# Encoder with seven-product feed-forward blocks: the first product of a pair is handed to the third one's bank by a copy on ScalarE

## The chip, the cores and the metric

The kernel runs on one core of one Trainium2 chip. The metric is the device time of one execution in microseconds, given as the median of three runs. A core has five engines that matter here: TensorE (PE) multiplies matrices and writes PSUM, VectorE (DVE), ScalarE (ACT) and GpSimd (POOL) work element by element, and SyncE (SP) issues most DMAs. Each has a queue of its own that it works through in order, and they wait for one another through semaphores.

## The reference

A two-layer encoder on 512 tokens of width 1024, in fp32. Each layer has two gated feed-forward blocks with an attention mixer and a cross-attention on 256 memory tokens between them:

```
def swiglu(x, wg, wu, wd):
    return (jax.nn.silu(x @ wg) * (x @ wu)) @ wd
...
for layer in range(2):
    g, wg, wu, wd = ffn1[layer]
    h = h + 0.5 * swiglu(rmsnorm(h, g), wg, wu, wd)
    ... h = h + mixer(rmsnorm(h, mix_g)), h = h + memory_xattn(rmsnorm(h, mg), rmsnorm(mem, sg))
    g, wg, wu, wd = ffn2[layer]
    h = h + 0.5 * swiglu(rmsnorm(h, g), wg, wu, wd)
```

The hidden width is 2816, which is 22 groups of 128 channels, worked on as 11 pairs of groups. Only the feed-forward blocks contain the change. There are four of them, at 0 to 330, 760 to 1050, 1050 to 1330 and 1740 to 2068 us of the span.

## The kernel before, in words

**Precision.** An fp32 operand is split in two parts of TensorE's fp32r type: a high part that ScalarE rounds (L457, `wh` or `sh`) and a low part that VectorE gets by subtraction (L458, `wl` or `sl`). A product is then three passes of matmuls, high x high, high x low, low x high. Tokens and hidden values have such parts too: `xh`, `t1h` to `t3h` and their low parts for the tokens, `hh` and `hl` (L379, L380) for the hidden values, `th` and `tl` (L385, L386) for sums of hidden values.

**Seven products.** The gate and up multiplication of a pair of hidden groups is done by the Strassen-Winograd scheme: the operands are cut in quarters, and seven products of quarters with some sums replace eight products. One product is `product` (L481), 24 matmuls of 128x256 into one PSUM bank of 128x512 fp32. Its two halves are gate and up. Pair 0 of each block, the plain pair, is done without the scheme (`plain_pair`, matmuls at L331), and pairs 1 to 10 in seven products. Where the text speaks of a block's first pair, pair 1 is meant, the first in seven products.

A pair p runs through these functions, each of which issues one or two products:
- `open_pair`: product with the tokens "11" into a fresh bank `y`. ScalarE copies it out to `gu` (L523).
- `sum_pair`: product with t1 into a bank `z`; product with t2, which accumulates on `y`. ScalarE copies `y` out (L541).
- `cross_pair`: product with the tokens "21" into a third bank `x`. VectorE adds `x` to the copy that L523 made (L550). Then a product with t3 accumulates on `y`, and ScalarE copies it out (L557), from which VectorE takes `z` (L558).
- `close_pair`: product with t4 on `y`, copied out at L574, and product "22" on `z`. VectorE multiplies by `R`, the factor of the rmsnorm (L609), ScalarE does the Silu (L610), VectorE multiplies by up (L611, L612). It is called after the next pair's `open_pair`.

`gu` is the result of a pair in SBUF, two tiles of 128x1024, one for each half of the tokens. `corner(pair, b, half)` is the piece for group b. There are four such tiles in all.

**The plain pair's end.** `plain_end` runs after the first `open_pair`: VectorE multiplies the two gate banks by `R` (L355), ScalarE does the Silu (L361), VectorE multiplies by the two up banks (L363).

**PSUM.** There are eight banks, four under the tag `pa` and four under `pb`. The plain pair holds three of `pa` (gate and up of its first group, gate of its second) and one of `pb`.

**Down projection.** It runs in three chunks of 8, 8 and 6 hidden groups. The second chunk, `down_seven`, is done in seven products too, in two units; `gain` (L628) adds each result to the residual stream `x` on VectorE, in two pieces of 128x256. It begins with the unit's first product, whose last quarter needs `hh` and `hl` of the newest pair. A unit's first, second and further products go through a bank `y`, and its third goes into a fresh bank `x`, as in `cross_pair`; `gain` runs after each of them. The other chunks (`down`, L707) are plain matmuls.

**What sets the order.** TensorE's order is the order of the program text. The other engines' instructions are placed by a scheduler from estimated times. `high_priority` brings an instruction forward in it, and `behind` puts one after a named other.

## Time and profile before

| | |
|---|---|
| median of three runs | 2066.76 us (2066.62 to 2070.43) |
| profiled execution, its own time | 2068.93 us |
| its span, first to last instruction | 2067.1 us |
| TensorE busy | 2027.3 us, 98% |
| VectorE busy | 1607.1 us, 78% |
| ScalarE busy | 1144.7 us, 55% |
| GpSimd busy | 375.3 us, 18% |
| granted TensorE clock, mean | 0.998 |

How to read it: all times inside the profile count from the span's start. "Busy" is time in which an engine works on an instruction, and a wait is idle time, put down to the instruction on another engine that released it. In the stretch views a row is the stretch, its length, then busy time and count of instructions for PE, PEld (TensorE's loading of weights), DVE, ACT and POOL, then the granted clock, the share of the DMA engines, and GB/s. In the waits a row is the waiting engine and line, what released it, and then the total in us, the count and the longest. In a timeline a row is start, length, engine and line, then what is written from what; a bracket gives idle time before it and the releaser.

### The profile page before, as it was taken

Reading aid. Unit: us, or ns where it says so; the run is one execution under the profiler, and the core shown is the slowest. Engines: PE = TensorE matmul, PEld = TensorE weight load, DVE = VectorE, ACT = ScalarE, POOL = GpSimd, SP = SyncE. Lnnn points to the kernel's source line nnn. Section 1 sums busy time; section 2 is a strip of 40 time slices with the busy share of each in tenths; the row PEclk is TensorE's granted clock in tenths of the full one; section 3 lists DMA queues with packets and bytes.
Section 4 is the critical chain, followed back from the end, with each engine's and each line's share of the span. In section 5 each row is a group of like instructions: output and inputs, shape, how many; then the busy total and the mean of one; then the engine's idle time right before and its main releaser. Section 6 shows DMA issues by size and latency. Waiting matters only on the chain.

```text
span 2067.1 us, 34071 instructions
## 1 busy us (share of the span) xinstructions
PE 2027.3 (98%) x13426; PEld 1836.5 (89%) x13426; DVE 1607.1 (78%) x2470; ACT 1144.7 (55%) x1718; POOL 375.3 (18%) x335
## 2 busy tenths in 40 slices
PE   8999999999999999999999999999999999999999
PEld 7989998887778889899989899988888888989997
DVE  8858987579876789599789679884668777958976
ACT  6525554465686565264555355454778665635543
POOL 1101003345432210000020000113453112000000
PEclk9999999999999999999999999999999999999999
DMA  7837565222232257376557465734223324746572
GB/s 229 214 112 184 163 166 179 94 77 72 67 128 77 72 161 213 103 197 161 156 156 191 133 173 145 211 124 154 82 88 120 100 81 125 194 130 175 162 193 95
DMA packets 89584, 292.32 MB, mean 141 GB/s; under 512 B 10064, under 2 KB 13264, under 8 KB 89424
## 3 DMA queue, kind: packets, MB, share of 16 engines
q1 hardware_dynamic: 75600, 239.81, 34.6%
q0 software_dynamic: 13824, 50.34, 13.9%
q8 instruction: 105, 1.72, 0.3%
q14 instruction: 55, 0.45, 0.1%
HBM read 283.82 MB, written 6.29 MB: 140 GB/s over the span
## 4 chain that ended last, share of the span: by engine, by line
PE 86%; DVE 9%; ACT 2%; issue 1%; DMA 1%; POOL 0%; SPq 0%; DVEq 0%; ACTq 0%; POOLq 0%
PE ps_pa L481 29%; PE ps_pb L481 12%; PE ps_pa L816 11%; PE ps_pa L707 6%; PE ps_pb L707 6%; PE ps_pa L767 4%; PE ps_pa L331 3%; PE ps_pb L922 2%; PE ps_pa L1362 2%; PE ps_pb L974 1%; PE ps_pa L1213 1%; PE ps_pb L767 1%; PE ps_pb L947 1%; DMA mem<-memT 1%; PE ps_pa L1132 1%
## 5 line engine op out<-in xcount | busy, mean ns | idle before, releaser
L164 ACT ACTIVATE wh<-wf 128x1024 fp32r<-128x1024 f32 (+2 forms) x179 | 181.2, 1014 | 250.2 <-PE ps_pa L707 68.5
L457 ACT ACTIVATE wh<-s 128x1024 fp32r<-128x1024 f32 x124 | 132.1, 1065 | 156.4 <-PE ps_pa L481 59.8
L166 DVE TENSOR_TENSOR wl<-wf,wh 128x1024 fp32r<-128x1024 f32 (+2 forms) x137 | 161.1, 1179 | 48.2 <-ACT wh L164 46.3
L458 DVE TENSOR_TENSOR wl<-s,wh 128x1024 fp32r<-128x1024 f32 x124 | 151.6, 1222 | 50.2 <-ACT wh L457 48.0
L457 ACT ACTIVATE wh<-wf 128x1024 fp32r<-128x1024 f32 x104 | 110.4, 1062 | 97.4 <-PE ps_pa L481 57.5
L458 DVE TENSOR_TENSOR wl<-wf,wh 128x1024 fp32r<-128x1024 f32 x104 | 126.9, 1220 | 8.2 <-ACT wh L457 3.7
L502 POOL DMA_DIRECT2D s<-l_ffn_wq x40 | 35.1, 878 | 519.5 <-DMA s<-l_ffn_wq 418.7
L166 POOL TENSOR_TENSOR wl<-wf,wh 128x1024 fp32r<-128x1024 f32 x42 | 101.9, 2425 | 150.9 <-ACT wh L164 140.3
L816 PE MATMUL ps_pa<-wh,xh 128*128 128x512 f32 x384 | 123.6, 403 | 0.0
L816 PE MATMUL ps_pa<-wh,xl 128*128 128x512 f32 x384 | 119.9, 394 | 0.0
L816 PE MATMUL ps_pa<-wl,xh 128*128 128x512 f32 x384 | 119.5, 392 | 0.0
L481 PE MATMUL ps_pa<-xh,wh 128*128 128x256 f32 x672 | 103.8, 276 | 0.0
L481 PE MATMUL ps_pa<-xh,wl 128*128 128x256 f32 x672 | 103.7, 276 | 0.0
L481 PE MATMUL ps_pa<-xl,wh 128*128 128x256 f32 x672 | 103.6, 276 | 0.0
L457 ACT ACTIVATE sh<-s 128x1024 fp32r<-128x1024 f32 x68 | 72.2, 1062 | 49.2 <-PE ps_pa L481 27.5
L231 POOL TENSOR_TENSOR acc<-acc,sq 128x512 f32<-128x512 f32 (+1 forms) x37 | 51.0, 1379 | 255.9 <-ACT sq L230 205.1
L458 DVE TENSOR_TENSOR sl<-s,sh 128x1024 fp32r<-128x1024 f32 x68 | 83.0, 1221 | 14.6 <-ACT sh L457 14.5
L481 PEld LDWEIGHTS ps_pa<-xh,wh 128*128 128x128 f32 x672 | 89.5, 188 | 0.6
L481 PEld LDWEIGHTS ps_pa<-xl,wh 128*128 128x128 f32 x672 | 88.8, 188 | 0.0
L481 PEld LDWEIGHTS ps_pa<-xh,wl 128*128 128x128 f32 x672 | 88.7, 188 | 0.0
L816 PEld LDWEIGHTS ps_pa<-wh,xl 128*128 128x128 f32 x384 | 72.9, 190 | 16.2
L816 PEld LDWEIGHTS ps_pa<-wl,xh 128*128 128x128 f32 x384 | 72.7, 189 | 16.0
(416 smaller groups left out, 5845.5 us busy)
## 6 DMA issues: line engine op xcount, KB each, us to landing
wf<-l_ffn_wq SPq DMA_DIRECT2D x120, 512.0 KB, 4.3
s<-l_ffn_wq SPq DMA_DIRECT2D x80, 512.0 KB, 5.5
s<-l_ffn_wq POOLq DMA_DIRECT2D x80, 512.0 KB, 7.3
wf<-l_w_in SPq DMA_DIRECT2D x48, 512.0 KB, 3.5
wf<-l_ffn_wd SPq DMA_DIRECT2D x32, 512.0 KB, 4.0
wf<-l_ffn_wdq SPq DMA_DIRECT2D x24, 512.0 KB, 3.4
wf<-l_ffn_wd SPq DMA_DIRECT2D x32, 384.0 KB, 3.1
s<-l_ffn_wdq SPq DMA_DIRECT2D x16, 512.0 KB, 4.9
```

Source lines behind the costliest of these rows:

```text
L164: self.leading = nc.scalar.activation(wh[:, sl], w[:, sl], AF.Copy)
L166: eng.tensor_sub(wl[:, sl], w[:, sl], wh.bitcast(F32)[:, sl])
L231: self.summed = (eng or nc.gpsimd).tensor_add(acc[:, :n], acc[:, :n], sq[:, :n])
L331: nc.tensor.matmul(p, w[a][:, k * P:(k + 1) * P], xs[k][c], start=k == order[0] and a == c == 0, stop=k == order[-1] and a == 1)
L457: self.leading = nc.scalar.activation(h, t, AF.Copy)
L458: self.parted = nc.vector.tensor_sub(l, t, h.bitcast(F32))
L481: self.nc.tensor.matmul(bank[:, sl], w[a][:, o:o + P], xs[k][b], start=first and z == a == b == k == 0, stop=z == a == 1 and k == KB // 2 - 1,
L707: self.nc.tensor.matmul(bank, w[a][:, j * P:(j + 1) * P], h, start=j == a == e == 0, stop=j == nb - 1 and (a, e) == ops[-1])
L767: nc.tensor.matmul(banks[dd], a[:, o:o + P], parts(k)[b], start=k == first and a is wh and b == 0, stop=k == last and a is wl)
L816: nc.tensor.matmul(banks[i], xs[k][a][:, i * P:(i + 1) * P], w[b][:, kk * 512:kk * 512 + 512], start=k == a == b == 0, stop=k == KB - 1 an ...
L922: nc.tensor.matmul(bank[:, o:o + n], a, b[:, :n], start=c == 0, stop=c == len(ops) - 1)
L1362: nc.tensor.matmul(p, ws[z][a][:, k * P:(k + 1) * P], xs[k][b], start=k == order[0] and a == b == 0, stop=k == order[-1] and a == 1)
```

## The change

In a pair, the first product's result is no longer copied to `gu` and added to there. ScalarE copies the bank `y` into a new bank `x` under the tag `pa`, right after the first product; the third product then accumulates on `x` instead of starting it; and ScalarE copies `x` to `gu`. VectorE's addition goes. Both `gu` tiles of a pair are now taken in `sum_pair`. In `down_seven` each unit's first result is copied to `x` in the same way, under the tag `pa` for the first unit and `pb` for the second, and `gain` is called once after the third product instead of after the first and the third. The diff, in full:

```diff
@@ -519,8 +519,8 @@
         pair.y = self.bank("pa")
         pair.w11, w = self.raw_operand(p, 0)
         self.product(pair.y, w, self.tokens("11"), True)
-        self.gu_half(pair)
-        self.nc.scalar.copy(self.corner(pair, 0, 0), self.halves(pair.y))
+        pair.x = self.bank("pa")
+        self.nc.scalar.copy(pair.x, pair.y)
         return pair
 
     def sum_pair(self, pair):
@@ -538,16 +538,15 @@
             f.lowered = self.parted
         self.product(pair.y, w, xs, False)
         self.gu_half(pair)
+        self.gu_half(pair)
         nc.scalar.copy(self.corner(pair, 0, 1), self.halves(pair.y))
 
     def cross_pair(self, pair, after=None):
         nc, f, p = self.nc, self.f, pair.p
         with self.behind(f.lowered if p == 1 else None):
             pair.w12, w = self.raw_operand(p, 1)
-        x = self.bank("pa")
-        self.product(x, w, self.tokens("21"), True)
-        c = self.corner(pair, 0, 0)
-        nc.vector.tensor_add(c, c, self.halves(x))
+        self.product(pair.x, w, self.tokens("21"), False)
+        nc.scalar.copy(self.corner(pair, 0, 0), self.halves(pair.x))
         if after is not None:
             self.full_sum(pair)
             after()
@@ -640,7 +639,9 @@
             units.append(t)
         for t in units:
             self.product(t.y, t.w, B["11"], False, range(n - 1, n))
-            self.gain(t.u, t.y, 0, 0)
+            t.x = self.bank("pb" if t.u else "pa")
+            with self.tc.high_priority():
+                nc.scalar.copy(t.x, t.y)
 
         def low(t):
             t.z = self.bank("pb")
@@ -656,10 +657,9 @@
             self.gain(t.u, t.y, 0, 1)
 
         def cross(t):
-            x = self.bank("pa")
             t.w12, w = self.raw_operand(t.p, 1)
-            self.product(x, w, B["21"], True)
-            self.gain(t.u, x, 0, 0)
+            self.product(t.x, w, B["21"], False)
+            self.gain(t.u, t.x, 0, 0)
 
         def left(t):
             w = self.left_sum(t.p)
```

TensorE's instructions and their order are the same, but for the tag of one bank in `down_seven`. The orders of SyncE and GpSimd are the same. Those of ScalarE and VectorE differ in the feed-forward blocks alone. Two places follow as the queues stand, the second on two engines. A row is the source line, the operation, what is written from what, its size, and in brackets the engines and DMA queues that it waits for. `s_384` and the like are sums of two weight quarters, loaded by DMA with addition; `wf` is a plain weight quarter. The line numbers of the changed kernel differ by one from L541 on (L542 for L541, L556 for L557).

ScalarE at the first pair of the first block, before:

```order
L457 ACTIVATE wh<-wf 128x1024 [waits DMAHW5_49,PE_49,Activation_49]
L523 COPY gu<-ps_pa 128x512 [waits PE_49]
L457 ACTIVATE sh<-s_384 128x1024 [waits DVE_49]
L457 ACTIVATE wh<-s_486 128x1024 [waits DMASW1_49,PE_49,Activation_49]
L457 ACTIVATE sh<-wf 128x1024 [waits DMAHW6_49,DVE_49,PE_49]
L541 COPY gu<-ps_pa 128x512 [waits PE_49]
L361 ACT_TABLE_LOAD
L361 ACTIVATE gs<-gs 128x1024 [waits DVE_49]
```

And in the changed kernel:

```order
L457 ACTIVATE wh<-wf 128x1024 [waits DMAHW5_49,PE_49,Activation_49]
L457 ACTIVATE sh<-s_384 128x1024 [waits DVE_49]
L457 ACTIVATE wh<-s_486 128x1024 [waits DMASW1_49,PE_49,Activation_49]
L523 COPY ps_pa<-ps_pa 128x512 [waits DVE_49]
L361 ACT_TABLE_LOAD
L361 ACTIVATE gs<-gs 128x1024 [waits DVE_49]
L457 ACTIVATE sh<-wf 128x1024 [waits DMAHW6_49,PE_49,Activation_49]
L542 COPY gu<-ps_pa 128x512 [waits PE_49]
```

The first result's copy stood behind one conversion and waited for TensorE alone; it now stands behind three, ahead of the Silu's table load, and waits for VectorE. In the other nine pairs it waits for TensorE.

VectorE at the start of `down_seven` in the second block, before (L377, L378, L382 and L383 make the sums `t` of hidden quarters, L653 a sum of weight quarters):

```order
L458 TENSOR_TENSOR wl<-wf,wh 128x1024 [waits DMAHW3_49,PE_49,Activation_49]
L377 TENSOR_TENSOR t<-gs 128x256 [waits DVE_49]
L550 TENSOR_TENSOR gu<-gu,ps_pa 128x512 [waits PE_49]
L458 TENSOR_TENSOR wl<-s_10028,wh 128x1024 [waits DMASW7_49,Activation_49]
L378 TENSOR_TENSOR gs<-gs 128x256 [waits DVE_49]
L653 TENSOR_TENSOR s_10028<-s_10028,wf 128x1024 [waits DVE_49]
L382 SCALAR_TENSOR_TENSOR t<-gs 128x256 [waits DVE_49]
L380 TENSOR_TENSOR hl<-gs,hh 128x1024 [waits Activation_49]
```

And in the changed kernel:

```order
L458 TENSOR_TENSOR wl<-wf,wh 128x1024 [waits DMAHW3_49,PE_49,Activation_49]
L377 TENSOR_TENSOR t<-gs 128x256 [waits DVE_49]
L378 TENSOR_TENSOR gs<-gs 128x256 [waits DVE_49]
L458 TENSOR_TENSOR wl<-s_10026,wh 128x1024 [waits DMASW7_49,PE_49,Activation_49]
L382 SCALAR_TENSOR_TENSOR t<-gs 128x256 [waits DVE_49]
L654 TENSOR_TENSOR s_10026<-s_10026,wf 128x1024 [waits DVE_49]
L380 TENSOR_TENSOR hl<-gs,hh 128x1024 [waits Activation_49]
L383 SCALAR_TENSOR_TENSOR t<-t,gs 128x256 [waits DVE_49]
```

The addition L550 and, some rows on, the additions of the first products are gone; L378 and L382 stand one or two places earlier, and `hl` still comes behind the sum of the weights. In the first block `hl` stands ahead of that sum in the changed kernel.

ScalarE at the same place, before:

```order
L541 COPY gu<-ps_pa 128x512 [waits PE_49]
L457 ACTIVATE wh<-s_10028 128x1024 [waits DMASW7_49,DVE_49,PE_49]
L379 ACTIVATE hh<-gs 128x1024 [waits DVE_49,Activation_49]
L385 ACTIVATE th<-t 128x768 [waits DVE_49]
L457 ACTIVATE sh<-s_10028 128x1024 [waits PE_49]
L457 ACTIVATE wh<-wf 128x1024 [waits DMAHW4_49,PE_49,Activation_49]
```

And in the changed kernel:

```order
L542 COPY gu<-ps_pa 128x512 [waits PE_49]
L457 ACTIVATE wh<-s_10026 128x1024 [waits DMASW7_49,PE_49,Activation_49]
L549 COPY gu<-ps_pa 128x512 [waits PE_49]
L379 ACTIVATE hh<-gs 128x1024 [waits DVE_49,Activation_49]
L385 ACTIVATE th<-t 128x768 [waits DVE_49]
L457 ACTIVATE sh<-s_10026 128x1024 [waits PE_49]
L644 COPY ps_pa<-ps_pa 128x512 [waits PE_49,Activation_49]
L457 ACTIVATE wh<-wf 128x1024 [waits DMAHW4_49,PE_49]
L644 COPY ps_pb<-ps_pa 128x512 [waits PE_49]
```

The copy of `x` to `gu` (L549) has come in ahead of `hh`, and the two copies of first products (L644) behind `th`.

## The prediction

> **What bounds the kernel now.** I began with the page's totals, then cut the span into its six stages, then asked TensorE alone what it waits for.

> ```profile
> span 2067.1 us, 34071 instructions
> PE 2027.3 (98%) x13426; PEld 1836.5 (89%) x13426; DVE 1607.1 (78%) x2470; ACT 1144.7 (55%) x1718; POOL 375.3 (18%) x335
> ```

> TensorE is busy for 98% of the span, and the change alters neither the number nor the shape of its matmuls. VectorE, which loses work, is at 78%, and its work is worth only what TensorE waits for it. So I look for the waits, and the stages in which they lie. The first column of the second view is the stretch, then its length, then busy time by engine.

> ```profile
> 0.00:330.00 330.00, 316.79 (x2392) 300.05 (x2393) 262.61 (x350) 173.62 (x214) 31.35 (x40) 1.00 0.62 174
> 760.00:1050.00 290.00, 288.76 (x2273) 277.53 (x2272) 235.92 (x290) 149.04 (x169) 18.65 (x21) 1.00 0.59 162
> ...
> PE ps_pa L481 <- DVE hl L380: 3.7, 4, 0.9
> PE ps_pa L481 <- ACT gu L541: 2.7, 1, 2.7
> ...
> PE ps_pa L481 <- ACT sh L457: 1.3, 1, 1.3
> ...
> PE ps_pa L481 <- DVE wl L458: 1.1, 4, 0.4
> ```

> L481 is the matmul of the seven-product scheme, the only code that the change touches. In the second feed-forward block (760 to 1050 us) TensorE is idle for 1.24 us of 290. In the whole run L481 waits 3.7 + 2.7 + 1.3 + 1.1 = 8.8 us. Nobody waits for the addition L550 or the first copy L523 on TensorE's side. Little can be won, then; the question is whether the change makes a wait.

> **What is removed and added.** The prices of the operations, minimum/median/maximum in ns:

> ```profile
> L523 ACT COPY gu<-ps_pa x40: 557/567/576, 35.6 to 2008.6; 128x512 f32<-128x512 f32 x40
> L550 DVE TENSOR_TENSOR gu<-gu,ps_pa x40: 678/680/689, 48.2 to 2022.2; 128x512 f32<-128x512 f32 x40
> L628 DVE TENSOR_TENSOR x<-x,ps_pa x80: 414/415/425, 233.8 to 1983.9; 128x256 f32<-128x256 f32 x80
> ```

> VectorE loses 40 additions of 0.68 us and 16 of the 80 + 32 pieces of 0.41 us at L628 (two units, two pieces, four blocks): 34 us. ScalarE gains 40 + 8 copies: 48 x 0.57 = 27 us, on an engine that is 55% busy. In the steady pairs both lie beside TensorE: a pair is seven products of 2.72 us, 19 us, with 11 to 13 us of ScalarE in it, so 0.57 us more fits; I cost them at zero there. If that cover were gone, 40 x 0.57 = 23 us would appear. The copy from PSUM into PSUM is in no row. Its nearest rows are L523 (same source, destination SBUF, 0.57) and, from the other side, L550's 0.68, which also ends a bank. I take 0.57, with 0.45 to 0.70 as bounds: four times 0.12 is 0.5 us in the sum.

> **Where a wait is made: the first pair of each block.** The first pair's copy needs a bank of the tag pa for the third product, ahead of its time. There are four. Three hold the plain pair's gate and up results, and the fourth the pair's own first product. The order of ScalarE says it: this copy waits for VectorE, all other pairs' copies for TensorE. The bank is freed by L355, the multiplication of a gate bank by R. The second block in order of time (columns: start, length in us, engine, line):

> ```profile
> 761.07 0.57 ACT L523 COPY gu<-ps_pa 128x512 f32<-128x512 f32 x1
> ...
> 763.48 0.62 PE L481 MATMUL ps_pa<-t2h,sh 128*128 128x256 f32 x4
> ...
> 765.67 1.28 DVE L355 TENSOR_TENSOR gs<-ps_pa,R 128x512 f32<-128x512 f32 x2
> ...
> 766.37 1.07 ACT L457 ACTIVATE sh<-wf 128x1024 fp32r<-128x1024 f32 x1 [2.02 <-DVE gs L355]
> ...
> 766.62 0.62 PE L481 MATMUL ps_pa<-xh,wh 128*128 128x256 f32 x4
> ...
> 769.34 0.62 PE L481 MATMUL ps_pa<-t3h,wh 128*128 128x256 f32 x4
> 769.34 1.22 DVE L458 TENSOR_TENSOR wl<-s,wh 128x1024 fp32r<-128x1024 f32 x1
> ...
> 770.61 0.73 PE L481 MATMUL ps_pa<-t3h,wl 128*128 128x256 f32 x4 [0.20 <-DVE wl L458]
> 771.18 0.63 PE L481 MATMUL ps_pa<-t3h,wh 128*128 128x256 f32 x4
> ```

> Today the first result is read out at 761.07, and the product with t2, which accumulates on the same bank, starts at 763.48. Tomorrow it must wait until the copy has read that bank. The copy starts when today's row at 766.37 does, which waits for the same L355, and TensorE follows. What such a release costs is seen in the first block, where a late copy of 0.56 us held L481:

> ```profile
> 169.53 0.56 ACT L541 COPY gu<-ps_pa 128x512 f32<-128x512 f32 x1
> ...
> 170.15 0.74 PE L481 MATMUL ps_pa<-t3h,sh 128*128 128x256 f32 x4 [2.73 <-ACT gu L541]
> ```

> TensorE starts 0.06 after the copy's end, and its first group takes 0.12 longer (0.74 instead of 0.62). So: 766.37 + 0.57 + 0.06 = 767.00; six groups take 769.34 - 766.62 = 2.72, plus 0.12; the next product starts at 769.84 instead of 766.62. That is 3.2 us late. VectorE's order up to L355 is the same as before, and ScalarE has nothing else ahead of the copy that ends later. The other three blocks, first row L355, second row the product behind t2:

> ```profile
> 39.90 1.28 DVE L355 TENSOR_TENSOR gs<-ps_pa,R 128x512 f32<-128x512 f32 x2
> ...
> 40.83 0.62 PE L481 MATMUL ps_pa<-xh,wh 128*128 128x256 f32 x4
> ...
> 1095.35 1.28 DVE L355 TENSOR_TENSOR gs<-ps_pa,R 128x512 f32<-128x512 f32 x2
> ...
> 1097.21 0.62 PE L481 MATMUL ps_pa<-xh,wh 128*128 128x256 f32 x4
> ...
> 1762.54 1.28 DVE L355 TENSOR_TENSOR gs<-ps_pa,R 128x512 f32<-128x512 f32 x2
> ...
> 1763.47 0.62 PE L481 MATMUL ps_pa<-xh,wh 128*128 128x256 f32 x4
> ```

> In the second block the way from L355's start to the next product is 769.84 - 765.67 = 4.17. So 39.90 + 4.17 - 40.83 = 3.2, 1095.35 + 4.17 - 1097.21 = 2.3, 1762.54 + 4.17 - 1763.47 = 3.2. Sum of the four: +12.0 us.

> Behind the waiting copy on ScalarE stand the table load, the Silu L361 and the next pair's conversion. The conversion needs a buffer that t2 reads, so it is late with TensorE and not because of the copy. Silu ends about 769.3, before VectorE's L363 uses it (row order, near 772). I cost these at nothing.

> What the delay takes away: in the product with t3, TensorE today loses time on wl (769.34 to 771.18 is 1.84 for three groups worth 1.36, so 0.48, of which 0.20 is the idle time shown). wl does not move, ending at 770.56, and t3 comes 2.3 to 3.2 us later. All four such waits go: 1.1 us of idle time in the view of waits, plus 4 x 0.28 for the restarts: -2.2 us.

> **The down projection in seven products.** Here TensorE waits four times for hl, the low part of the last hidden pair. The second block:

> ```profile
> 946.93 1.06 ACT L457 ACTIVATE wh<-s 128x1024 fp32r<-128x1024 f32 x1 [1.13 <-PE ps_pa L481]
> ...
> 947.31 0.42 DVE L377 TENSOR_TENSOR t<-gs 128x256 f32<-128x256 f32 x1
> ...
> 947.65 0.68 DVE L550 TENSOR_TENSOR gu<-gu,ps_pa 128x512 f32<-128x512 f32 x1
> ...
> 951.19 1.22 DVE L380 TENSOR_TENSOR hl<-gs,hh 128x1024 fp32r<-128x1024 f32 x1
> 951.26 0.28 PE L481 MATMUL ps_pa<-hh,sh 128*128 128x256 f32 x1
> ...
> 952.46 0.38 PE L481 MATMUL ps_pa<-hl,sh 128*128 128x256 f32 x1 [0.92 <-DVE hl L380]
> ```

> Only one matmul at 951.26 can run, and the next, due about 0.1 later, starts at 952.46: 1.1 us lost, 1.2 with the restart. L550 stands in that chain and is removed, and L378 moves to its place, ahead of wl. In the new order the chain is bounded by wh: it ends at 947.99, so wl starts at 948.05. Steps of 1.14 for wl and the sum s, 0.34 for L382 put hl at 950.67 to 951.89, against 952.41 today: 0.5 us won. In the first block hl stands ahead of s, and hh (wh's end 947.99 + copy 0.57 + 1.06 = 949.6) lets it run from about 949.65 to 950.9, before it is needed: 1.2 won. Sum -(1.2 + 3 x 0.5) = -2.7 us. The two new copies of first products must end before the second step; by that order the first ends near 954.9, and the second step starts after 956, so no wait.

> **The clock.** The trace shows what gaps can do to TensorE. In two stretches the column before the last two, the granted clock, falls:

> ```profile
> 496.00:500.00 4.00, 4.00 (x15) 3.25 (x13) 3.89 (x11) 2.34 (x4) 3.49 (x3) 0.57 0.02 4
> 544.00:548.00 4.00, 4.00 (x16) 3.30 (x15) 3.32 (x8) 3.00 (x5) 0.07 (x1) 0.57 0.00 0
> ...
> 169.00:173.00 4.00, 2.85 (x25) 2.85 (x26) 4.00 (x7) 2.56 (x4) 0.88 (x1) 1.00 0.26 101
> ```

> Both lose 4 x 0.43 = 1.7 us, and both follow stretches in attention where TensorE ran only a few transposes. After the 2.73 us wait at 170 the clock stayed at 1.00. The new waits of 3.2 us lie between. I put half a window, 0.9 us, into the sum, with none and three as bounds. [...]

> **Sum.** +12.0 - 2.2 - 2.7 + 0.9 = +8.0 us. Against the profiled execution's 2068.93 that is 2076.9; that execution is 2.2 above the median of the runs, so against the median, 2066.76, it is 2074.8, +0.39%. About 0.2% (4.1 us) is what a measurement of this kernel can tell from no change.

> **Rivals.**
> - Half clock after all three long waits: +7.1 + 3 x 1.7 = +12.2, 2079.0. For it speaks the length of the waits, against it the 2.73 that did nothing.
> - The delay is partly given back in the first block. There L481 waits 2.7 and 1.3 us for ScalarE, which stands behind loads of the memory tokens. If those loads come at fixed times, a pipeline that is 3 us later no longer waits: 4.0 and 2 x 0.28 for restarts, so +8.0 - 4.6 = +3.4, 2070.2. Against it: these loads wait in turn for buffers that the same pipeline frees.
> - ScalarE becomes late in every pair: 40 x 0.57 = 23 more, 2097. Against it 55% load; for it that x's second copy stands ahead of hh in ScalarE's order.
> - The other side: the first copy finds a bank free, as if the plain pair's results had been read out before 763.48, and hl is in time in all four blocks: -4 x 1.2 = -4.8, 2062.0. It is decided by when L355 ends; it ends after t2's start in all four blocks, so I hold it for nearly excluded.

> **Chances.** The forecast 0.62, three slow windows 0.15, given back 0.13, late ScalarE 0.05, the other side 0.03, something else 0.02. The likeliest gives 2074.8, its own range being 2072 to 2078. The range 2070 to 2080 takes in the first two rivals and both ends of the copy's price. Slower 0.83, within 0.2% 0.13, faster 0.04.

> **What the new profile would show.** TensorE's L481 waiting for the copy of L523, four times, 2.3 to 3.4 us each, about 12 in total; the waits on wl gone; the wait for hl smaller, with the first block's gone; SyncE and GpSimd as before. I am wrong if that first wait is missing or under 2 us, if ScalarE's copies hold TensorE in other pairs, or if the copy into PSUM takes far from 0.57.

## The result, and the profile after

The changed kernel takes 2080.69 us (median of 4 runs, 2079.89 to 2082.8), against 2068.6 for the kernel before (median of 4): a ratio of 1.006, 95% interval 1.0042 to 1.0077. It is slower by some 12 us, where 8 were forecast, and the time lies just above the range. (The forecast time stood on a median of 2066.76 for the kernel before; from 2068.6 the same 8 us lead to 2076.6.) The two profiled executions differ by 12.2 us in span, 2079.3 against 2067.1. Of all the runs in this document one lies far off: of the twelve of the kernel with the first pair as before, the profiled one took 11681 us, and it is left out of that kernel's ratio, its trace out of the eleven used below.

The page's totals of the changed kernel:

```profile
span 2079.3 us, 34073 instructions
PE 2033.5 (98%) x13426; PEld 1843.3 (89%) x13426; DVE 1587.0 (76%) x2414; ACT 1170.3 (56%) x1766; POOL 375.3 (18%) x335
```

VectorE is busy for 20 us less and ScalarE for 26 us more. (VectorE's instructions together are 33 us shorter, as forecast; in the record neighbours overlap: in the changed kernel `sl` of L458 runs from 765.59 to 766.81, and `wl` behind it starts at 766.72.) TensorE has the same 13426 matmuls and is busy for 6 us longer, which no count of instructions explains: some of them ran slower (a group of four took up to 1.23 us, below). The waits of L481:

```profile
PE ps_pa L481 <- ACT ps_pa L523: 11.5, 4, 3.4
PE ps_pa L481 <- ACT gu L542: 2.0, 1, 2.0
PE ps_pa L481 <- DVE hl L380: 1.3, 3, 0.4
PE ps_pa L481 <- ACT wh L457: 0.7, 1, 0.7
...
PE ps_pa L481 <- DVE sl L458: 0.3, 1, 0.3
```

The line of the copy by itself, with its duration as minimum/median/maximum in ns, and what it waited for (us, times):

```profile
L523 ACT COPY ps_pa<-ps_pa x40: 570/580/591, 39.9 to 2020.8; 128x512 f32<-128x512 f32 x40
...
  DVE gs L355: 6.3, 4
```

Four waits on the copy of a first result have appeared, and the copy itself waited four times for L355. The waits on wl (1.1 us) are gone, and those on hl fell from 3.7 to 1.3. The copy from PSUM into PSUM takes 0.58. In time order, the second block's first pair, and behind it TensorE's row after the wait in the first, the third and the fourth block:

```profile
767.86 1.28 DVE L355 TENSOR_TENSOR gs<-ps_pa,R 128x512 f32<-128x512 f32 x2
768.58 0.57 ACT L523 COPY ps_pa<-ps_pa 128x512 f32<-128x512 f32 x1 [2.08 <-DVE gs L355]
...
769.20 1.22 PE L481 MATMUL ps_pa<-t2h,sh 128*128 128x256 f32 x4 [3.39 <-ACT ps_pa L523]
...
40.51 0.74 PE L481 MATMUL ps_pa<-t2h,sh 128*128 128x256 f32 x4 [3.00 <-ACT ps_pa L523]
...
1102.46 0.72 PE L481 MATMUL ps_pa<-t2h,sh 128*128 128x256 f32 x4 [2.04 <-ACT ps_pa L523]
...
1772.31 1.23 PE L481 MATMUL ps_pa<-t2h,sh 128*128 128x256 f32 x4 [3.12 <-ACT ps_pa L523]
```

This is the chain that was forecast: L355, the copy 0.72 behind its start, TensorE 0.05 behind the copy's end. But in the second and the fourth block the first group after it takes 1.22 us, not the 0.74 that a group after a wait took before. The stretches around the four places tell why. Each pair of rows is a stretch of 3.41 us with the wait or most of it, and the one behind; the columns are again busy times of PE, PEld, DVE, ACT and POOL, then the granted clock, third from the end:

```profile
38.24:41.65 3.41, 1.14 (x9) 1.15 (x10) 3.41 (x5) 1.75 (x2) 0.00 (x0) 1.00 0.05 18
41.65:45.06 3.41, 3.41 (x18) 3.41 (x17) 3.41 (x6) 1.93 (x3) 0.00 (x0) 0.50 0.01 2
765.28:768.69 3.41, 0.53 (x5) 0.33 (x3) 3.41 (x5) 1.17 (x2) 0.00 (x0) 1.00 0.79 234
768.69:772.10 3.41, 2.90 (x13) 2.90 (x14) 3.41 (x7) 2.80 (x3) 0.00 (x0) 0.50 0.00 0
1099.79:1103.20 3.41, 1.37 (x12) 1.17 (x11) 3.41 (x5) 2.39 (x3) 0.00 (x0) 1.00 0.01 5
1103.20:1106.61 3.41, 3.41 (x18) 3.41 (x18) 3.41 (x7) 0.34 (x2) 0.00 (x0) 0.50 0.02 5
1768.80:1772.21 3.41, 0.39 (x4) 0.19 (x2) 3.41 (x5) 1.58 (x2) 0.00 (x0) 1.00 0.72 219
1772.21:1775.62 3.41, 3.31 (x15) 3.31 (x16) 3.41 (x7) 2.38 (x3) 0.00 (x0) 0.50 0.01 4
```

At all four places TensorE runs for 3.41 us at half clock, even behind the shortest, of 2.04 us in the third block.

Where the 12.2 us lie can be read off by setting each TensorE row of after beside the same row of before and taking the difference of their starts. Starts of the first row of the t2 product, and of the first row behind it:

| block | t2, before | t2, after | later, without the shift that stood | next product, before | next product, after | added within t2 |
|---|---|---|---|---|---|---|
| 1 | 38.08 | 40.51 | 3.17 | 40.83 | 44.85 | 1.59 |
| 2 | 763.48 | 769.20 | 3.55 | 766.62 | 773.38 | 1.04 |
| 3 | 1094.49 | 1102.46 | 2.20 | 1097.21 | 1106.90 | 1.72 |
| 4 | 1760.50 | 1772.31 | 3.28 | 1763.47 | 1776.69 | 1.41 |
| sum | | | 12.2 | | | 5.8 |

The shifts that stood, read at the row just ahead of t2, are -0.74, 2.17, 5.77 and 8.53 (after later than before, where positive). The rest: -1.58 in the t3 products of the first three blocks, -2.16 at hl in them, -1.02 for both in the fourth, -1.5 in the first block beside that, +0.1 at its end, +1.1 in the attention of layer 0 (two stretches of 3.41 us at half clock in a row at 495.6 instead of one), -0.74 at the start. Together 12.2.

### The profile page after: what moved, and what is told of

It reads as the page before. It is cut to its first block, busy times and chain, and to the rows that moved or that the text cites. A ratio compares the mean times of both kernels' runs of the same rounds, so it can differ in the third digit from the quotient of the medians.

```text
span 2079.3 us, 34073 instructions
## 1 busy us (share of the span) xinstructions
PE 2033.5 (98%) x13426; PEld 1843.3 (89%) x13426; DVE 1587.0 (76%) x2414; ACT 1170.3 (56%) x1766; POOL 375.3 (18%) x335
## 3 DMA queue, kind: packets, MB, share of 16 engines
q8 instruction: 105, 1.72, 0.3%
## 4 chain that ended last, share of the span: by engine, by line
PE 86%; DVE 8%; ACT 2%; DMA 2%; issue 2%; POOL 1%; SPq 0%; ACTq 0%; POOLq 0%; DVEq 0%
PE ps_pa L481 29%; PE ps_pb L481 12%; PE ps_pa L816 11%; PE ps_pa L707 6%; PE ps_pb L707 6%; PE ps_pa L767 4%; PE ps_pa L331 2%; PE ps_pb L922 2%; PE ps_pa L1362 2%; PE ps_pb L974 1%; PE ps_pa L1213 1%; PE ps_pb L947 1%; PE ps_pb L767 1%; PE ps_pa L1132 1%; DVE xl L214 1%
## 5 line engine op out<-in xcount | busy, mean ns | idle before, releaser
L457 ACT ACTIVATE wh<-s 128x1024 fp32r<-128x1024 f32 x124 | 132.0, 1065 | 130.2 <-PE ps_pa L481 49.0
L166 DVE TENSOR_TENSOR wl<-wf,wh 128x1024 fp32r<-128x1024 f32 (+2 forms) x137 | 161.1, 1179 | 48.8 <-ACT wh L164 46.8
L458 DVE TENSOR_TENSOR wl<-s,wh 128x1024 fp32r<-128x1024 f32 x124 | 151.6, 1223 | 60.5 <-ACT wh L457 58.0
L457 ACT ACTIVATE wh<-wf 128x1024 fp32r<-128x1024 f32 x104 | 110.7, 1064 | 94.7 <-PE ps_pa L481 40.8
L458 DVE TENSOR_TENSOR wl<-wf,wh 128x1024 fp32r<-128x1024 f32 x104 | 127.0, 1222 | 20.0 <-ACT wh L457 15.1
L166 POOL TENSOR_TENSOR wl<-wf,wh 128x1024 fp32r<-128x1024 f32 x42 | 101.8, 2424 | 151.9 <-ACT wh L164 141.3
L457 ACT ACTIVATE sh<-s 128x1024 fp32r<-128x1024 f32 x68 | 72.3, 1064 | 61.3 <-PE ps_pa L481 33.1
L458 DVE TENSOR_TENSOR sl<-s,sh 128x1024 fp32r<-128x1024 f32 x68 | 83.4, 1226 | 30.2 <-ACT sh L457 30.1
L481 PE MATMUL ps_pa<-xh,wh 128*128 128x256 f32 x672 | 103.9, 277 | 0.0
L481 PE MATMUL ps_pa<-xh,wl 128*128 128x256 f32 x672 | 103.8, 276 | 0.0
L481 PE MATMUL ps_pa<-xl,wh 128*128 128x256 f32 x672 | 103.6, 276 | 0.0
L481 PEld LDWEIGHTS ps_pa<-xh,wh 128*128 128x128 f32 x672 | 89.7, 188 | 0.6
L481 PEld LDWEIGHTS ps_pa<-xl,wh 128*128 128x128 f32 x672 | 88.8, 188 | 0.0
L481 PEld LDWEIGHTS ps_pa<-xh,wl 128*128 128x128 f32 x672 | 88.8, 188 | 0.0
```

The lines of the kernel that those rows point to most:

```text
L166: eng.tensor_sub(wl[:, sl], w[:, sl], wh.bitcast(F32)[:, sl])
L457: self.leading = nc.scalar.activation(h, t, AF.Copy)
L458: self.parted = nc.vector.tensor_sub(l, t, h.bitcast(F32))
L481: self.nc.tensor.matmul(bank[:, sl], w[a][:, o:o + P], xs[k][b], start=first and z == a == b == k == 0, stop=z == a == 1 and k == KB // 2 - 1,
```

## Experiments

The ratios below are to runs of the kernel before that were taken with each group of kernels; their medians were 2069.82 us for the kernels with the free bank, with the first pair as before, with the down projection alone and with L355 earlier, 2070.44 for the last two with shorter waits, and 2069.05 for the others.

**The bank.** The first pair's `x` is taken where a bank is free; the condition on `mem_r` holds in the first block alone:

```diff
-        pair.x = self.bank("pa")
+        pair.x = self.bank("pb" if p == 1 else "pa")
+        if p == 1 and self.mem_r is None:
+            for z in range(2):
+                self.nc.tensor.matmul(pair.x[:, z * 256:z * 256 + 256], w[0][:, :P], self.tokens("11")[0][0],
+                                      start=z == 0, stop=z == 1, skip_group_check=True)
```

> The changed kernel, but the first pair's x comes from the tag pb, where a bank is free, so that its copy need not wait for L355 (in the first block two extra matmuls write that bank ahead of the copy, about 0.5 us). Theory, the missing bank: the four waits on the copy (11.5 us) and the four half-clock windows behind them go, the waits on wl (1.1 us) come back, the wait for hl stays at about 1.3 us; -2.7 us against before plus 0.5 for the two matmuls, 2066.4 against 2068.6. Rival, the copies themselves: a copy in each pair disturbs TensorE or the clock wherever the bank comes from, and the time stays near 2080. Rival in part: only the waits go and the clock still falls, about 2071.

Measured: 2067.03 us, a ratio to before of 0.9987 (0.9979 to 0.9996), the forecast having been 0.9989. No wait on the copy is left in the trace, and none of the first pairs has a window at half clock. So all of the loss hung on that bank, its clock included, and 40 + 8 copies by themselves cost nothing that shows in an interval of 0.0017, 3.5 us. (A wait of 2.6 us behind the memory tokens, which the kernel before has too, has a half-clock window behind it here, at 171.5.)

**The first pair as before.** The rest of the change is kept:

```diff
+        if p == 1:
+            self.gu_half(pair)
+            self.nc.scalar.copy(self.corner(pair, 0, 0), self.halves(pair.y))
+            return pair
         pair.x = self.bank("pa")
...
+        if p == 1:
+            x = self.bank("pa")
+            self.product(x, w, self.tokens("21"), True)
+            c = self.corner(pair, 0, 0)
+            nc.vector.tensor_add(c, c, self.halves(x))
+        else:
             self.product(pair.x, w, self.tokens("21"), False)
```

> The changed kernel, but the first pair of each block is done as before (first result copied to gu, VectorE's addition); the other 36 pairs and the seven-product down projection as changed. Theory, the missing bank: no wait on the first copy, no half-clock window in the feed-forward blocks, hl's wait about 1.3 us, so 2.7 us below before: 2065.9 against 2068.6. Rival, the cost lies in every pair: about 36/40 of the 12 us stay, 2079.

Measured: 2065.9 us (median of the twelve), 0.998 (0.9971 to 0.9988), against the forecast 0.9987. It is faster than before, and its median is the lowest here, though its interval overlaps with that of the free bank. The same kernel once more, for its trace:

> The kernel with the first pair of each block as before and the rest as changed, once more for its trace. Theory: no wait on a first copy in any block, the waits on wl 1.1 us and on hl 1.3 us in all, no half-clock window behind the first pairs, in the first block a wait of 1.3 to 2.8 us on the copy behind the memory tokens.

One run of 2068.04 us. Its waits of L481:

```profile
PE ps_pa L481 <- ACT gu L547: 2.3, 1, 2.3
PE ps_pa L481 <- DVE hl L380: 1.3, 3, 0.4
PE ps_pa L481 <- DVE wl L458: 0.9, 3, 0.4
```

As expected, with one exception: in the first block the clock fell behind the wait of 2.3 us on the copy that stands behind the memory tokens, a wait that the kernel before has as well, with 2.73 us and at full clock. That, as in the kernel with the free bank, needed explaining, and the last four kernels below are about it.

**The two halves of the change.** First the down projection alone (the diff's two hunks in `down_seven`, on the kernel before):

> The kernel before with the change made in the seven-product down projection alone. Theory: the wait for hl shrank because L550 left VectorE's chain ahead of it and not because of gain, so the waits on hl stay near 3.7 us and the time is that of before within 1 us, 2067.6 to 2069.6. Rival: the removed pieces of gain are what shortened it, -2.4 us; or the new copies hold TensorE there, +1 to +5 us.

Measured: 2068.57 us, 0.9995 (0.9986 to 1.0003), no difference that can be told.

```profile
PE ps_pa L481 <- DVE hl L380: 3.7, 4, 0.9
```

The wait on hl is as before, to the digit. So the removed pieces of `gain` did not shorten it in the changed kernel, and the two new copies hold nothing up there: they have no row among the waits. Then the pairs alone (the other hunks):

> The kernel before with the change made in the pairs alone, the seven-product down projection as before. Theory: all of the loss is in the pairs' first copy, so the waits on it stay at 2.0 to 3.4 us, 11.5 in all, the waits on hl are 1.3 to 2 us since L550 is gone, and the time is that of the changed kernel, 2079 to 2083 against 2069. Rival: the two copies in the down projection carry a part of the loss, and the time is 2075 to 2078.

Measured: 2083.11 us, 1.0064 (1.005 to 1.0077), all of the loss.

```profile
PE ps_pa L481 <- ACT ps_pa L523: 12.3, 4, 3.8
...
PE ps_pa L481 <- DVE hl L380: 1.3, 3, 0.4
```

The shorter wait on hl comes with this half. That it is the missing L550 in VectorE's queue, and not another shift of order in the same half, is read from the queues and was not tried by itself. Behind two of the four waits, at 769.24 and 1772.75, the half clock lasted two stretches of 3.41 us here, and in the third block there was none.

**L355 earlier.** The wait is made shorter with nothing else taken away; `f.gated` is L355:

```diff
         with self.tc.high_priority():
             f.lowered = nc.vector.tensor_add(pair.s, pair.s, pair.w11)
             xs = self.tokens("2")
-            w = self.operand(pair.s)
+            with self.behind(f.gated if p == 1 else None):
+                w = self.operand(pair.s)
```

> The changed kernel with VectorE's two multiplications L355 put ahead of the two conversions that stood before them, so that the bank comes free 2.3 us earlier and the wait on the copy shrinks from 2.0 to 3.4 us to about 1.2 to 1.5. Theory, the clock falls only when most of one window of its grid of 3.41 us is idle (2.04 us idle in one window was enough, 1.37 was not): four waits of 1.2 to 1.5, 5.4 us in all, no half-clock window behind them, about 2068.6 + 5.4 - 1.7 - 2.7 = 2069.6, 2068 to 2071. Rival, any wait of over 1 us brings the clock down: four windows of 1.3 more, 2075.

Measured: 2068.77 us, 0.9996 (0.9987 to 1.0004), where 1.0005 was expected.

```profile
PE ps_pa L481 <- ACT ps_pa L523: 3.7, 3, 1.2
```

Three waits of 1.2 are left where four were expected, in the third block none, and no window at half clock stands behind them. So moving two multiplications of 0.64 us by two places takes back the loss against the kernel before: 7.8 us of waiting, and the clock with it.

**What brings the clock down.** Waits on purpose, in the kernel before, in 28 places, ahead of the t3 product:

```diff
+        n = {2: 1440, 3: 1600, 5: 1760, 6: 1920, 7: 2080, 9: 2240, 10: 2400}.get(p)
+        if n:
+            c = self.corner(pair, 0, 1)[:, 0]
+            spare = f.tp.tile([P, 240], F32R, name="spare", tag="spare", bufs=1)
+            with self.tc.high_priority():
+                for i in range(0, n, 240):
+                    m = min(240, n - i)
+                    nc.gpsimd.tensor_sub(spare[:, :m], c[:, :m], c[:, :m])
+            nc.tensor.matmul(pair.y[:, :256], spare[:, :P], self.tokens("3")[0][0], start=False, stop=False,
+                             skip_group_check=True)
         self.product(pair.y, w, self.tokens("3"), False)
```

> The kernel before with a wait made on purpose in 28 places (pairs 2, 3, 5, 6, 7, 9 and 10 of each block): GpSimd makes zeros from the pair's second result, 1440 to 2400 columns in steps of 160, and one matmul of zeros ahead of the t3 product waits for them. By GpSimd's 2.4 ns a column the waits should be some 1.2 to 3.5 us. Question: what decides whether the clock falls behind a wait. Theory, the share of one window of the fixed grid of 3.41 us that is idle: no wait below 1.4 us brings it down, all above 3.4 do, and between them it goes by where the grid's line cuts the wait, so that some of 2.0 us gate and some of 2.7 don't; the bound lies between 1.4 and 2.0 us idle in one window; some 16 of 28 waits, 28 x 2.35 + 16 x 1.7 = 93 us more, 2162. Rival, the length alone: a bound in us above which every wait gates and below which none does, wherever it lies. Rival, a full idle window: only waits of over 3.4 us gate, 66 + 4 x 1.7 = 73 more, 2142.

> As the kernel with 28 waits made on purpose, with the lengths in the opposite order over the pairs (2400 columns in pair 2 down to 1440 in pair 10), so that other lengths meet other positions of the grid. Theory, idle share of one window: the same bound between 1.4 and 2.0 us idle in one window separates the waits that gate from those that don't. Rival, the length alone: the same bound in us of the whole wait in both kernels.

Measured: 2349.13 and 2349.05 us, far more than expected, since the waits came out at 7.5 us on average:

```profile
PE ps_pa L563 <- POOL spare L562: 201.1, 27, 9.1
```

The first of them on GpSimd, in time order:

```profile
62.12 7.50 POOL L562 TENSOR_TENSOR spare<-gu 128x240 fp32r<-128x240 f32 x5 [2.20 <-ACT gu L541]
```

The five pieces taken apart, with GpSimd's busy time alone behind the length of the stretch (the last two pieces are as the third):

```profile
62.10:64.78 2.68, 2.64 (x1) 1.00 0.93 240
64.82:67.64 2.82, 2.79 (x1) 0.64 0.76 272
67.69:68.30 0.61, 0.59 (x1) 0.50 0.91 349
```

They follow each other with less than 0.1 us between, so it is not the waiting of each for the one before that makes the chain long. Three pieces take 0.59, close to the 0.57 that I had worked out from one long operation (L166 on GpSimd, 128x1024 in 2.43 us in the kernel before), and the first two over four times as much. Beside those two VectorE was busy for 2.63 and 2.35 us, beside the other three not at all. Over the whole trace, 73 pieces of 240 columns beside which VectorE worked for less than a fifth of the time took 0.61 us on average, and 98 beside which it worked for over four fifths took 1.17 (0.65 to 2.79). That VectorE's work is the cause was not tried. Waits so long fill a whole window of the grid nearly everywhere, and the two kernels do not tell the theories apart. Two more were shorter, 720 to 1120 columns:

> As the kernel with 28 waits made on purpose, but shorter: 720 to 1120 columns over the pairs. The two kernels before gave 4.8 us for 1440 columns and 1.13 us for each further 240, so 720 should wait 1.4, 800 1.75, 840 1.95, 880 2.15, 960 2.5, 1040 2.9 and 1120 3.3 us. Theory, the idle share of one window of the grid: idle of 1.67 us in a window did not gate in the traces so far, of 1.96 and more did; no wait of 1.4 gates, some 40% of those between 1.95 and 2.5 don't, since the grid cuts them in two, nearly all of 3.3 do; 14 or 15 of 28; 64 us of waits, 10 for the matmuls of zeros and restarts, 25 for the clock: 2168. Rival, the length alone: one bound in us, the same for every place, with 12 to 24 waits gating; the sum can be the same, and the table of single waits tells it apart: under this rival no longer wait stays at full clock while a shorter one loses it.

> The same with the lengths in the opposite order over the pairs. Theory, the idle share of one window: the same length that gates in one place doesn't in another, by where the grid's line falls; between 1.67 and 1.96 us idle in one window the answer changes. Rival, the length alone: the same lengths gate as in the kernel with the first order.

Measured: 2239.53 and 2244.45 us. The waits, 4.0 us on average, were still longer than worked out: pieces of 240 columns took 1.1 us on average, and in at least 16 places an issue of a DMA, some 0.9 us, stands between two pieces. But the second kernel has the waits that decide. Two of them, in the first block:

```profile
323.44 0.39 PE L563 MATMUL ps_pa<-t3h,spare 128*128 128x256 f32 x1 [3.61 <-POOL spare L562]
345.62 0.58 PE L563 MATMUL ps_pa<-t3h,spare 128*128 128x256 f32 x1 [2.74 <-POOL spare L562]
```

And their windows, cut at the lines of this run's grid:

```profile
318.30:321.71 3.41, 1.53 (x14) 1.33 (x12) 3.35 (x4) 2.06 (x2) 3.18 (x3) 1.00 0.01 2
321.71:325.13 3.42, 1.69 (x14) 1.69 (x15) 0.83 (x1) 0.00 (x0) 1.59 (x2) 1.00 0.38 115
325.13:328.54 3.41, 3.41 (x32) 3.41 (x31) 1.29 (x2) 1.55 (x2) 0.00 (x0) 1.00 0.00 0
...
342.19:345.60 3.41, 0.69 (x7) 0.50 (x5) 3.26 (x4) 0.96 (x2) 3.22 (x3) 1.00 0.00 0
345.60:349.01 3.41, 3.39 (x16) 3.39 (x17) 0.25 (x1) 0.00 (x0) 0.00 (x0) 0.50 0.42 120
```

The wait of 3.61 us is cut in two by a line at 321.71, leaves 1.88 and 1.72 us of idle time in two windows, and the clock stays. The wait of 2.74 us lies inside one window, and the next runs at half. The length alone is refuted as the rule: the longer wait kept the clock and the shorter one lost it. The kernel with the pairs alone shows the same in the third block's first pair, where its wait of 2.04 us is as long as the changed kernel's:

```profile
1105.05 0.73 PE L481 MATMUL ps_pa<-t2h,sh 128*128 128x256 f32 x4 [2.04 <-ACT ps_pa L523]
```

Its windows:

```profile
1100.33:1103.74 3.41, 2.67 (x24) 2.48 (x22) 3.31 (x5) 2.12 (x3) 0.00 (x0) 1.00 0.47 154
1103.74:1107.15 3.41, 2.10 (x18) 2.10 (x19) 3.41 (x8) 1.63 (x2) 0.00 (x0) 1.00 0.02 5
1107.15:1110.56 3.41, 3.41 (x32) 3.41 (x32) 3.41 (x5) 1.54 (x2) 0.00 (x0) 1.00 0.25 62
```

There a line at 1103.74 leaves 0.74 us of idle time on one side and 1.31 on the other, and the clock stays at 1.00. And the old wait of 2.73 us at 170 us in the kernel before is of that kind too:

```profile
165.37:168.78 3.41, 2.04 (x17) 1.84 (x16) 1.68 (x3) 1.47 (x3) 0.73 (x1) 1.00 0.75 202
168.78:172.20 3.42, 2.05 (x18) 2.06 (x19) 3.42 (x6) 2.28 (x3) 0.33 (x1) 1.00 0.33 131
```

All windows of the grid at full clock in the feed-forward blocks of the eleven traces, from the window behind TensorE's first matmul on, by TensorE's idle time in them, and how many had half clock in the next:

| idle in one window, us | windows | half clock next |
|---|---|---|
| 1.00 to 1.72 | 20 | 0 |
| 1.74 to 1.94 | 7 | 2 |
| 1.95 to 3.41 | 117 | 117 |

The rows are cut where the counts change. The bound is a little over half a window, and blurred between 1.74 and 1.95; the ends of matmuls in the trace are modelled, which may be why. The window of the first matmul itself is outside the table: in the kernel before, 2.74 us of the window at 4.94 were idle, and the record has 1.00 behind it, though 9 matmuls took the 3.42 us of the next window and 16 the 3.41 us of the one after. In the attention stages, where the matmuls are transposes and small pieces, the same table does not hold (in the changed kernel 1.91 us idle at 540.00 kept the clock, 1.53 at 543.41 lost it); I did not look into why.

## Why the prediction was wrong

Its direction and its mechanism were right; one term was mis-sized.

- **The wait on the bank**: +12.0 forecast, at 3.2, 3.2, 2.3 and 3.2; these are delays of the product behind t2, restart and all. For the start of t2 itself the same working (L355's start + 0.70 + 0.57 + 0.06) gives 3.15, 3.52, 2.19 and 3.37; measured 3.17, 3.55, 2.20 and 3.28, 12.2 in both sums. Shown by the two kernels that remove the cause (another bank, the first pair as before) and by the one that frees the bank earlier.
- **The clock, the step that failed**: "I put half a window, 0.9 us, into the sum, with none and three as bounds." Measured: all four. The product behind t2 starts 12.2 + 5.8 = 18.0 us late in the four blocks together, where the wait alone was worth 12.0 by the forecast, whose starts of t2 came true, so the clock cost 6.0 us. (Half of TensorE's busy time in the four slow stretches, 13.03 / 2 = 6.5, is about the same.) So this term was 5.1 us too small; the first block and the profiled pair's other differences gave 1.0 back. Between the forecast time and the measured one there are also the 1.8 us by which the median of the kernel before moved. The reason given for the 0.9 was one wait of 2.73 us that did nothing. I read it as a bound on the length. It was luck: 1.37 us of it lay in one window and 1.36 in the next. The two old windows at half clock pointed to a grid, had I subtracted them: 544.25 - 496.46 = 47.79 = 14 x 3.413. With that grid, and with the bound of 1.95 us that only the later kernels gave, a wait of 3.2 us has a part of over 1.95 us on one side of a line in 1 - (2 x 1.95 - 3.2)/3.41 = 79% of its positions, and 2.3 us in 53%; with some 1.7 us for each, half of 3.41, the term was worth, as an estimate, 3 x 0.79 x 1.7 + 0.53 x 1.7 = 4.9 us. The rival with a slow window after the three long waits (+12.2, 2079.0) is the nearest to what happened.
- **The waits on wl and hl**: -2.2 - 2.7 = -4.9 forecast, -4.8 measured (1.58 + 2.16 + 1.02). That hl gains by the half of the change in which L550 goes is shown: 3.7 us without that half, 1.3 with it; L550 itself is argued.
- **The steady pairs and the down projection's copies at zero**: shown within the noise, by the free bank (0.9987) and by the down projection alone (0.9995).
- **The delay given back in the first block**: it held at most in part. The wait of 1.27 us on sh vanished and the one behind the memory tokens fell from 2.73 to 1.99, while one on wh grew by 0.5; 1.5 us in all instead of the 4.6 of that rival. Even this is not shown to come from the delay: with the down projection alone, where the first pairs are as before, there is no wait on sh either and the one behind the memory tokens is 1.3, and with L355 earlier it is 2.8.
- **The attention**: 1.1 us of the difference lie in a stage whose instructions the change does not touch, by one more window at half clock. The position of the grid differs from trace to trace (its lines lie 1.53 us past the multiples of 3.4133 in the kernel before, 0.69 in the changed one), and the down projection alone and L355 earlier, neither of which has a half-clock window in the feed-forward blocks, have such a second window in this stage too (at 492.5 and 540.7). So I count this as chance in the profiled pair and not as an effect; the runs of the kernel before scatter over 4 us (2066.62 to 2070.75).

## What to carry to other kernels

A copy that hands a result to a later accumulation needs its bank earlier than the product did (four waits here, 11.5 us): count the banks held at that moment in every stage, the start of a block above all, and look at which read frees the next one. A TensorE wait of over about 2 us in a dense stretch of matmuls like these should be priced at its length plus 1.7 us times the chance that it fills a little more than half of one clock window of 3.41 us (1.95 us idle and more in the table above, 117 of 117), not at its length alone; and 1.7 is one window, where two of the waits in the kernel with the pairs alone cost two. And an operation that hides its own cost everywhere else can be kept: done as before in 4 of 40 pairs, the change is 0.2% faster than the kernel before (ratio 0.9971 to 0.9988).

## What was not expected of the hardware

GpSimd's subtraction of 128x240 took 0.59 us where VectorE was idle beside it and up to 2.79 where VectorE was busy, both in the trace of the first kernel with waits on purpose.
